# Attention's value projection as seven block products in a hand-written order

## The chip, the cores and the metric

One core of one Trainium2 chip runs the whole program. The metric is device time in microseconds (us) of one execution; lower is better. TensorE (PE) multiplies, VectorE (DVE), ScalarE (ACT) and GpSimd (POOL) do elementwise work, SyncE (SP) issues the transfers.

## The reference

Two pre-normalised residual layers on x of 512 frames by 1024 channels, each with a token mixer and a gated MLP. The first layer's mixer is a pooling mixer, the second's is attention of 16 heads of 64.

```python
for i in range(DEPTH):                      # DEPTH = 2
    h = rmsnorm(x, mix_norm[i])
    x = x + (pool_mixer if i == 0 else chunk_attention)(h, ...)
    h = rmsnorm(x, ffn_norm[i])
    x = x + (silu(causal_dwconv3(h @ w_gate)) * (h @ w_val)) @ w_out   # d_ff = 2816
...
qkv = h @ w_qkv                             # [512, 1024] x [1024, 3072]
q, k, v = jnp.split(qkv, 3, axis=-1)        # q and k are normalised by head
```

The change concerns v = h @ w_v, a product of 512 x 1024 by 1024 x 1024, and what stands just ahead of it and just behind it.

## The kernel before

Activations lie channel-major in `X[0..7]`, eight tiles of 128 channels by 512 frames in fp32. Every fp32 product is made from three products of rounded parts (`mm3`, lines 121 to 125): an operand is split into hi, a rounded copy made by ACT, and lo, the remainder made by DVE (`split`, lines 97 to 103; `split_scaled`, lines 105 to 108, the same with a scale), and hi x hi, hi x lo and lo x hi are added in PSUM. A matmul has a stationary operand of 128 x 128 and a moving one of 128 x 512.

**The end of the first layer.** `ffn` (line 382) makes the 2816 hidden channels in 22 tiles, most of them with seven block products in place of eight (`strassen`), and adds the output product in four groups of hidden tiles (`OUT`). The last group, `output(3)`, has five hidden tiles; for each of the eight output tiles d it makes 15 matmuls, for which a 128 x 640 weight is loaded, split (lines 409 and 410, one tile ahead) and consumed, and DVE adds the result onto `X[d]` (line 833). The hidden rows' two parts lie in slots `U`: four pairs in a pool and eight in `set1`. The groups take turns at two halves of `U`.

**The opening of attention.** `prepare` scales `X[k]` by the norm's gain and splits it into `XS` (which is `set2`, in the tiles `two`; lines 107 and 108), squares it on ACT (line 146) and lets POOL add the squares into `n_acc` (line 148). The factor of each frame is applied later, to the results. `project(0)` makes the first four heads' q and k in four PSUM banks with 96 matmuls, its weights loaded in four pieces of 512 KB (`load_split`). Then come the frames' factors (`frame_rstd`), the head norms, and four multiplications on POOL that apply them to `Z` (line 979). `values(0)` and `values(1)` make the halves of v, 96 matmuls each: for each of four pieces of 256 channels, eight groups of three matmuls, in which the lo part of the weights is used from the second matmul on. `evict` scales and splits the results out of PSUM into `set1`, 16 small steps on ACT and as many on DVE for each half (lines 107 and 108, tiles `one`). `channel_major(0, i)` transposes `Z` on PE, splits it and moves it by DMA. Then the heads begin, with the three other projections woven in; their lo parts are made by POOL (`project(1)`, line 103 on POOL).

**What sets the order.** Within `manual_schedule` an engine's instructions keep the order in which they are written. Before, that holds for PE in `ffn` and in the heads, and for DVE, ACT and SP in the middle of `ffn`; the opening of attention, and the output products of the last group on ACT and DVE, are ordered by a planner from priorities and estimated times. Weights' parts of all stages take turns in two buffers for hi and two for lo (`wh`, `wl`), loads in three (`wr`).

## Time and profile before

| what | value |
|---|---|
| median of 3 runs | 972.0 us (971.98 to 972.19) |
| the profiled execution's own time | 972.12 us |
| its span, from the first to the last instruction | 970.3 us |
| PE busy | 961.6 us, 99% of the span |
| PE's weight loads (PEld) | 815.0 us, 84% |
| DVE busy | 809.6 us, 83% |
| ACT busy | 576.6 us, 59% |
| POOL busy | 102.9 us, 11% |

Rows of the timeline give the start in us, the duration in us, the engine, the source line, the operation, output <- inputs, and the count; in brackets the idle time before it and what ended it. Rows that follow each other and are alike may be merged (x4), and a few matmuls are missing from a trace. A matmul's duration reaches over the start of the next one: the distance between starts is what one costs.

### The profile page before, as it was taken

What the parts mean: (1) busy time and instruction counts of PE and PEld (TensorE: products, weight loads), DVE (VectorE), ACT (ScalarE), POOL (GpSimd) and SP (SyncE); (2) the same over time, 40 slices, a digit from 0 to 9 for tenths busy, and PEclk for the clock granted to TensorE, in tenths of its full rate; (3) what the DMA queues carried; (4) which work ended last, traced back from release to release, by engine and by line L of the source; (5) the groups of instructions that cost most, each with busy time, mean ns of one, the idle gap of its engine ahead of it and who ended that gap; (6) DMA issues with size and microseconds to landing.
All of it is one profiled execution on the core that took longest, in us unless ns stands there. A gap on an engine that the chain in (4) does not pass through costs nothing.

```text
span 970.3 us, 13704 instructions
## 1 busy us (share of the span) xinstructions
PE 961.6 (99%) x4982; PEld 815.0 (84%) x4982; DVE 809.6 (83%) x1462; ACT 576.6 (59%) x990; POOL 102.9 (11%) x90
## 2 busy tenths in 40 slices
PE   8999999999999999999999999999999999999998
PEld 7788988888888888888888787888988888888886
DVE  8999999999899854442777888999999999989953
ACT  7665564655555544345898988646565565566531
POOL 2300000000000013204534532000000000000000
PEclk9999999999999999999999999999999999999999
DMA  9222332332323224232343341332233233332323
GB/s 342 77 93 71 114 113 75 120 120 92 105 76 120 78 84 147 94 121 91 111 115 107 97 118 55 101 108 80 94 114 104 87 120 108 104 103 77 116 79 109
DMA packets 37427, 102.82 MB, mean 106 GB/s; under 512 B 4432, under 2 KB 7904, under 8 KB 37360
## 3 DMA queue, kind: packets, MB, share of 16 engines
q1 hardware_dynamic: 37296, 101.90, 33.0%
q8 instruction: 39, 0.64, 0.3%
q14 instruction: 28, 0.23, 0.1%
q0 software_dynamic: 32, 0.04, 0.0%
q10 hardware_dynamic: 32, 0.00, 0.0%
HBM read 95.60 MB, written 2.14 MB: 101 GB/s over the span
## 4 chain that ended last, share of the span: by engine, by line
PE 94%; DVE 4%; ACT 2%; issue 0%; DMA 0%; DVEq 0%; ACTq 0%
PE st_m L610 11%; PE out L124 8%; PE out L123 8%; PE out L125 8%; PE st_m L612 6%; PE st_t L610 6%; PE gv L124 4%; PE gv L123 4%; PE gv L125 4%; PE qk L124 3%; PE qk L123 3%; PE qk L125 3%; PE st_t L612 3%; PE st_b L610 3%; PE tp L1078 2%; PE oo L1090 2%
## 5 line engine op out<-in xcount | busy, mean ns | idle before, releaser
L124 PE MATMUL out<-one,ow_h 128*128 128x512 f32 x224 | 87.9, 393 | 0.0
L123 PE MATMUL out<-one,ow_h 128*128 128x512 f32 x224 | 87.8, 392 | 0.0
L125 PE MATMUL out<-one,ow_l 128*128 128x512 f32 x224 | 87.8, 392 | 0.0
L833 DVE TENSOR_TENSOR X<-out,X 128x512 f32<-128x512 f32 (+1 forms) x65 | 44.1, 680 | 49.1 <-PE out L125 48.9
L409 ACT ACTIVATE ow_h<-wo_r 128x640 fp32r<-128x640 f32 (+1 forms) x64 | 50.4, 788 | 56.4 <-PE out L124 46.8
L610 PE MATMUL st_m<-two,g_h 128*128 128x512 f32 x240 | 75.1, 394 | 0.0
L610 PE MATMUL st_m<-h,g_h 128*128 128x512 f32 x240 | 74.0, 389 | 0.0
L410 DVE TENSOR_TENSOR ow_l<-wo_r,ow_h 128x640 fp32r<-128x640 f32 (+1 forms) x64 | 56.5, 883 | 2.5 <-ACT ow_h L409 2.5
L424 DVE SCALAR_TENSOR_TENSOR c<-a,col,c 128x511 f32<-128x511 f32 (+1 forms) x76 | 56.3, 743 | 0.0
L610 PEld LDWEIGHTS st_m<-h,g_h 128*128 128x128 f32 x240 | 45.1, 188 | 10.3
L612 PEld LDWEIGHTS st_m<-two,g_l 128*128 128x128 f32 x240 | 45.0, 188 | 9.5
L610 PEld LDWEIGHTS st_m<-two,g_h 128*128 128x128 f32 x240 | 44.0, 188 | 10.4 <-ACT w L619 0.8
L619 ACT ACTIVATE w<-st_m 128x512 f32<-128x512 f32 x30 | 17.9, 598 | 56.8 <-PE st_m L612 56.8
L125 PE MATMUL qk<-wqk_h,two 128*128 128x512 f32 x128 | 51.4, 402 | 0.0
L123 PE MATMUL qk<-wqk_h,two 128*128 128x512 f32 x128 | 50.8, 409 | 0.0
L124 PE MATMUL qk<-wqk_l,two 128*128 128x512 f32 x128 | 50.8, 397 | 0.0
L612 PE MATMUL st_m<-h,g_l 128*128 128x256 f32 x240 | 48.3, 283 | 0.0
L125 PEld LDWEIGHTS out<-one,ow_l 128*128 128x128 f32 x224 | 42.3, 189 | 6.3
L124 PEld LDWEIGHTS out<-one,ow_h 128*128 128x128 f32 x224 | 42.3, 189 | 6.3 <-DVE one L435 0.3
L612 PE MATMUL st_m<-two,g_l 128*128 128x256 f32 x240 | 47.6, 280 | 0.0
L123 PEld LDWEIGHTS out<-one,ow_h 128*128 128x128 f32 x224 | 42.3, 189 | 6.0
L1066 DVE CUSTOM_DVE_ANT_0 sb<-sc,B 128x128 f32<-128x128 f32 (+1 forms) x64 | 31.1, 486 | 18.9 <-PE sc L1063 18.1
(378 smaller groups left out, 2928.6 us busy)
## 6 DMA issues: line engine op xcount, KB each, us to landing
gv_r<-gv SPq DMA_DIRECT2D x86, 512.0 KB, 3.9
wo_r<-wout SPq DMA_DIRECT2D x32, 384.0 KB, 3.1
wo_r<-wout SPq DMA_DIRECT2D x32, 320.0 KB, 2.9
wqk_r<-wqk SPq DMA_DIRECT2D x16, 512.0 KB, 3.4
wv_r<-wv SPq DMA_DIRECT2D x8, 512.0 KB, 3.3
wo_r<-wo SPq DMA_DIRECT2D x8, 512.0 KB, 3.4
xt<-xt SPq DMA_DIRECT2D x4, 512.0 KB, 5.1
X<-xT SPq DMA_DIRECT2D x8, 256.0 KB, 7.4
```

Of the source, the lines that this page charges most:

```text
L123: yield nc.tensor.matmul(o, sh, mh, start=first, stop=False, **how)
L124: yield nc.tensor.matmul(o, sh, ml, start=False, stop=False, **how)
L125: yield nc.tensor.matmul(o, sl, mh, start=False, stop=last, **how)
L409: nc.scalar.activation(hi[:, :n], raw[:, :n], AF.Copy)
L410: return hi, lo, lambda: nc.vector.tensor_sub(lo[:, :n], raw[:, :n], hi[:, :n].bitcast(F32))
L424: nc.vector.scalar_tensor_tensor(c[:, j:], a[:, :S - j], cw[2 - j], c[:, j:], op0=OP.mult, op1=OP.add)
L610: nc.tensor.matmul(o, hi[:, c], B[i, name], start=first and i == 0, stop=False, **how)
L612: nc.tensor.matmul(o[:, 0], lo[:, c], B[i, name][:, 0], start=False, stop=i == 3, **how)
L833: nc.vector.tensor_add(X[d][:, fs], o[:, fs], X[d][:, fs])
L1066: nc.vector.tensor_tensor_reduce(out=s_[:, :n], in0=sc[:, :n], in1=BT[h % 2][:, :n][:, ::-1], scale=1.0, scalar=3e38, op0=OP.add, op1=OP.m ...
L1078: nc.tensor.transpose(tp[:, j * P:(j + 1) * P], s_[:, j * P:(j + 1) * P], ident)
L1090: nc.tensor.matmul(oo[:, j * P:], V[j, h // 4][:, h % 4].rearrange("p a d -> p (a d)"), PT[e][c][:, 4 * j:3 * j + TT].rearrange("p t q -> ...
```

## The change

The 1024 x 1024 product is cut into blocks of two by two: frames into halves (256 each), channels into even and odd tiles of 128, output columns into halves of 512. Seven block products take the place of eight (Winograd's form). Their left sides are a11, a12, a22 and four sums s1 to s4 of blocks of the scaled activations; their right sides are b11, b21 and b22, and four differences t1 to t4 of blocks of the weights, made by DVE in the loaded tiles. b22 is loaded a second time, since t2 is made in its place.

- The sums s1 to s4 (`frame_sums`, on DVE, 256 frames wide) and their parts (`forms_hi`, `forms_lo`) are made between the last output products of the first layer, through a hook in `output` (`after`, `amid`). `ffn` returns before the last group's products, and `opening` runs them. The parts go into `set1`, so the groups of the first layer's `ffn` take their slots the other way round, and the last one uses the pool's four pairs, which now lie in a pool of their own.
- The scaled activations get an fp32 copy (`Y`), from which hi is made. The squares are added by DVE and no longer by POOL.
- Each product is made in two halves of 12 matmuls (`half`): 8 with the hi part of the weights, then 4 with the lo part.
- Results are added up in SBUF (`x1`, `y6`, `y5`, `c12`) and from there scaled and split into `set1` (`store`).
- One order is written out for PE, DVE, ACT and SP, from the last output products to the last store.
- Pools: weight blocks and sums lie in a pool (`pre`) that closes ahead of the heads' tiles; three pools wait tile by tile.

The functions `frame_sums`, `forms_hi`, `half`, `after` and the order that is written out:

```diff
-    def prepare(XS, c, name):
-        acc = g_tile(f"{name}_acc")
-        for k in range(KD):
-            split_scaled(X[k], col[:, c + k:c + k + 1], XS[k], XS[KD + k])
-        for k in range(KD):
-            sumsq(k, acc, name)
...
+    def ffn(l, first, pool, acc, summed=None, upool=None, hook=None):
+        U = [tuple((upool or pool).tile([P, S], F32R, name=f"u{j}{c}") for c in "hl") for j in range(2 * GM - KD)]
         U += [(set1[j], set1[KD + j]) for j in range(KD)]
-        slot = {f: U[f - b + GM * (g % 2)] for g, (b, n) in enumerate(OUT) for f in range(b, b + n)}
+        slot = {f: U[f - b + GM * (g % 2 if hook is None else 1 - g % 2)] for g, (b, n) in enumerate(OUT) for f in range(b, b + n)}
...
+            last = hook is not None and g == len(OUT) - 1
             def halves(d):
-                w.append(parts(asked.pop((g, d)), m * P, f"ow{l}_{g}_{d}", True, True))
+                raw = asked.pop((g, d))
+                if last:
+                    hi, lo = (wp.tile([P, 1024], F32R, name=f"ow{l}_{g}_{d}_{c}", tag=f"w{c}", bufs=2) for c in "hl")
+                    nc.scalar.activation(hi[:, :m * P], raw[:, :m * P], AF.Copy)
+                    w.append((hi, lo, lambda: nc.vector.tensor_sub(lo[:, :m * P], raw[:, :m * P], hi[:, :m * P].bitcast(F32))))
+                else:
+                    w.append(parts(raw, m * P, f"ow{l}_{g}_{d}", True, True))
...
+                if last and d:
+                    hook["after"](d - 1)
                 o = psum("Q", f"out{l}_{g}_{d}")
                 for i in range(m):
+                    if last and i == 2:
+                        hook["amid"](d)
...
+            PAIRS, ONE, FOUR = ((4, 5), (10, 11), (14, 15), (0, 1)), (9, 12, 13, 8), (2, 3, 6, 7)
+            halves = slice(0, HALF), slice(HALF, S)
+            def scaled(k):
+                Y[k] = g_tile(f"y{k}")
+                nc.scalar.activation(Y[k], X[k], AF.Copy, scale=gain(k))
+                nc.scalar.activation(XS[k], Y[k], AF.Copy)
+                SQ[k] = g_tile(f"n1_sq{k}")
+                nc.scalar.activation(SQ[k], X[k], AF.Square)
+            def low(k):
+                nc.vector.scalar_tensor_tensor(XS[KD + k], X[k], gain(k), XS[k].bitcast(F32), op0=OP.mult, op1=OP.subtract)
+            def add_square(k):
+                nc.vector.tensor_add(SQ[0], SQ[0], SQ.pop(k))
+            def frame_sums(m):
+                ye, yo = Y.pop(2 * m), Y.pop(2 * m + 1)
+                (a11, a21), (a12, a22) = ([y[:, h] for h in halves] for y in (ye, yo))
+                sums[m] = vx(f"s23_{m}"), vx(f"s14_{m}")
+                (s2, s3), (s1, s4) = ([x[:, h] for h in halves] for x in sums[m])
+                nc.vector.tensor_add(s1, a21, a22)
+                nc.vector.tensor_sub(s3, a11, a21)
+                nc.vector.tensor_sub(s2, s1, a11)
+                nc.vector.tensor_sub(s4, a12, s2)
+            def forms_hi(m):
+                s23, s14 = sums[m]
+                h23, l23 = (set1[j] for j in PAIRS[m])
+                one, four = set1[ONE[m]], set1[FOUR[m]]
+                nc.scalar.activation(h23, s23, AF.Copy)
+                for x, h in zip((one, four), halves):
+                    nc.scalar.activation(x[:, :HALF], s14[:, h], AF.Copy)
+                form["s2", m], form["s3", m] = ((h23[:, h], l23[:, h]) for h in halves)
+                form["s1", m], form["s4", m] = ((x[:, :HALF], x[:, HALF:]) for x in (one, four))
+            def forms_lo(m):
+                s23, s14 = sums.pop(m)
+                h23, l23 = (set1[j] for j in PAIRS[m])
+                nc.vector.tensor_sub(l23, s23, h23.bitcast(F32))
+                for x, h in zip((set1[ONE[m]], set1[FOUR[m]]), halves):
+                    nc.vector.tensor_sub(x[:, HALF:], s14[:, h], x[:, :HALF].bitcast(F32))
...
+            def part_hi(key):
+                part[key] = [wp.tile([P, 1024], F32R, name=f"{key}_{c}", tag=f"w{c}", bufs=2) for c in "hl"]
+                nc.scalar.activation(part[key][0], raws[key], AF.Copy)
+            def part_lo(key):
+                nc.vector.tensor_sub(part[key][1], raws[key], part[key][0].bitcast(F32))
...
+            def t4(j):
+                nc.vector.tensor_sub(blocks["b21", j], blocks["b21", j], blocks["b22", j])
+            SEQ = ("b11", "b21", "b22", "b11", "b12", "b21", "b22")
...
+            def after(d):
+                if d in (3, 5):
+                    forms_hi((d - 3) // 2)
+                scaled(d)
+                if d == 6:
+                    part_hi("q0")
+                if d == 1:
+                    low(0)
+                if d == 2:
+                    low(1)
+                if d > 1:
+                    add_square(d - 1)
+                if d in (2, 4, 6):
+                    frame_sums(d // 2 - 1)
+                if d in (3, 5):
+                    forms_lo((d - 3) // 2)
+                if 3 < d < KD - 1:
+                    ask(d - 4)
+                if d > 3:
+                    for n in (("b11", "b12"), ("b22",), ())[d - 4]:
+                        for j in range(2):
+                            block(n, j)
+            def amid(d):
+                if d == KD - 1:
+                    part_lo("q0")
+            hook["after"], hook["amid"] = after, amid
+            run(rest)
...
+            def half(n, o, name, first):
+                z, j = divmod(n, 2)
+                h, l = part.pop(f"v{n}")
+                how = {"skip_group_check": not first}
+                for c in range(2):
+                    s = slice(c * S, (c + 1) * S)
+                    for i in range(2):
+                        sh, sl = stationary(name, 2 * j + c, i)
+                        nc.tensor.matmul(o[i], sh, h[:, s], start=first and n % 2 == 0 and c == 0, stop=False, **how)
+                        nc.tensor.matmul(o[i], sl, h[:, s], start=False, stop=False, **how)
+                for i in range(2):
+                    for c in range(2):
+                        sh, _ = stationary(name, 2 * j + c, i)
+                        nc.tensor.matmul(o[i], sh, l[:, c * S:(c + 1) * S], start=False, stop=j == 1 and c == 1, **how)
+            forms_hi(2)
+            ask(3)
+            for j in range(2):
+                block("b21", j)
+            part_hi("q1")
+            scaled(7)
+            low(2)
+            low(3)
+            part_lo("q1")
+            add_square(6)
+            forms_lo(2)
+            add_square(7)
+            frame_sums(3)
+            project(0)
+            part_hi("q2")
+            forms_hi(3)
+            low(4)
+            low(5)
+            part_lo("q2")
+            forms_lo(3)
+            t1(0)
+            project(1)
+            part_hi("q3")
+            low(6)
+            low(7)
+            part_lo("q3")
+            t1(1)
+            t2(0)
+            project(2)
+            st = psum("P", "n1_st")
+            for t in range(TT):
+                nc.tensor.matmul(st[:, t:t + 1], SQ[0][:, t * P:(t + 1) * P], ones, start=True, stop=True)
+            a, rcol, t_ = (small(f"n1_{c}", TT) for c in "ayt")
+            nc.vector.tensor_scalar(a, st[:, :TT], 1.0 / D, EPS, op0=OP.mult, op1=OP.add)
+            nc.scalar.activation(t_, a, AF.Ln)
+            nc.scalar.activation(rcol, t_, AF.Exp, scale=-0.5)
+            hi(0)
+            t2(1)
+            nc.vector.scalar_tensor_tensor(t_, rcol, -0.5, rcol, op0=OP.mult, op1=OP.mult)
+            nc.vector.tensor_mul(t_, t_, a)
+            nc.vector.scalar_tensor_tensor(rcol, t_, 1.5, rcol, op0=OP.add, op1=OP.mult)
+            nc.vector.scalar_tensor_tensor(r2, rcol, 1.0 / HD, rcol, op0=OP.mult, op1=OP.mult)
+            lo(0)
+            project(3)
...
+            def store(src, t, h):
+                for hh in range(2):
+                    V[t, 2 * h + hh] = vt = set1[(t * 2 + h) * 2 + hh].rearrange("p (h a d) -> p h a d", h=4, a=2)
+                    v4 = src[:, hh * 256:(hh + 1) * 256].rearrange("p (h d) -> p h d", d=HD)
+                    for e in range(2):
+                        split_scaled(v4[:, e::2, :], rcol[:, t:t + 1], vt[:, e::2, e, :], vt[:, e::2, 1 - e, :])
...
+            hi(1)
+            nc.vector.tensor_copy(flat[1], ov[1])
+            nc.scalar.activation(flat[0], ov[0], AF.Copy)
+            nc.scalar.activation(flat[2], ov[2], AF.Copy)
+            nc.vector.tensor_copy(flat[3], ov[3])
+            square(0)
+            lo(1)
+            half(0, A, "a11", True)
+            hi(2)
+            for t in range(1, TT):
+                square(t)
+            reduce(0)
+            lo(2)
+            reduce(1)
+            t3(0)
+            half(1, A, "a11", True)
+            x1 = pair_of("x1")
+            for i in range(2):
+                copy(x1, A, i)
+            hi(3)
+            reduce(2)
+            reduce(3)
+            lo(3)
+            nc.vector.tensor_mul(by_frame(a), by_frame(ss), r2[:, :, None].to_broadcast([P, TT, 8]))
+            nc.vector.tensor_scalar(a, a, EPS, None, op0=OP.add)
+            B = [psum("P", f"vb{i}") for i in range(2)]
+            half(2, B, "a12", True)
+            hi(4)
+            nc.scalar.activation(t_, a, AF.Ln)
+            nc.scalar.activation(y, t_, AF.Exp, scale=-0.5)
+            lo(4)
+            t3(1)
+            nc.vector.scalar_tensor_tensor(t_, y, -0.5, y, op0=OP.mult, op1=OP.mult)
+            nc.vector.tensor_mul(t_, t_, a)
+            nc.vector.scalar_tensor_tensor(y, t_, 1.5, y, op0=OP.add, op1=OP.mult)
+            nc.vector.tensor_mul(by_frame(y), by_frame(y), rcol[:, :, None].to_broadcast([P, TT, 8]))
+            for t in range(TT):
+                nc.gpsimd.tensor_mul(Z[0, t], Z[0, t], by_frame(y)[:, t, :, None].to_broadcast([P, 8, HD]))
+            half(3, B, "a12", True)
+            hi(5)
+            lo(5)
+            add(x1, B)
+            half(4, A, "s2", False)
+            hi(6)
+            lo(6)
+            t4(0)
+            half(5, A, "s2", False)
+            hi(7)
+            y6 = pair_of("y6")
+            for i in range(2):
+                copy(y6, A, i)
+            lo(7)
+            t4(1)
+            C = [psum("S", f"vc{i}", 4) for i in range(2)]
+            half(6, C, "s3", True)
+            hi(8)
+            lo(8)
+            for j in range(2):
+                blocks["b22", j] = load(source(1, 1, j), f"b22r_{j}")
+            channel_major(0, 0)
+            half(7, C, "s3", True)
+            hi(9)
+            lo(9)
+            channel_major(0, 1)
+            add(y6, C)
+            store(x1[0], 0, 0)
+            half(8, A, "s1", False)
+            hi(10)
+            lo(10)
+            store(x1[1], 1, 0)
+            half(9, A, "s1", False)
+            hi(11)
+            y5 = pair_of("y5")
+            for i in range(2):
+                copy(y5, A, i)
+            lo(11)
+            B = [psum("P", f"vd{i}") for i in range(2)]
+            half(10, B, "a22", True)
+            hi(12)
+            lo(12)
+            add(y5, C)
+            store(y5[0], 2, 1)
+            half(11, B, "a22", True)
+            hi(13)
+            lo(13)
+            add(y6, B)
+            store(y5[1], 3, 1)
+            half(12, A, "s4", False)
+            store(y6[0], 2, 0)
+            half(13, A, "s4", False)
+            c = pair_of("c12")
+            nc.scalar.activation(c[0], A[0], AF.Copy)
+            nc.vector.tensor_copy(c[1], A[1])
+            store(y6[1], 3, 0)
+            for i in range(2):
+                store(c[i], i, 1)
+            return rcol
...
-            yield from products(ov, wqk[c], f"wqk{c}", nc.gpsimd if c else None, evict)
-            if c == 0:
-                rcol = frame_rstd(acc, "n1")[0]
-                nc.vector.scalar_tensor_tensor(r2, rcol, 1.0 / HD, rcol, op0=OP.mult, op1=OP.mult)
+            yield from products(ov, wqk[c], f"wqk{c}", nc.gpsimd, evict)
...
-        def values(half, banks):
...
-        run(project(0, "SS"))
-        while late:
-            late.pop(0)()
-        run(values(0, "PQ"))
-        for i in range(2):
-            channel_major(0, i)
-        run(values(1, "SS"))
+        r2, late = small("r2", TT), []
+        closing = ExitStack()
+        with tc.tile_pool(name="pre", bufs=1, reuse_waits="tile") as pre:
+            with tc.manual_schedule(engines={ET.PE, ET.DVE, ET.Activation, ET.SP}):
+                rcol = opening(pre)
...
+    hidden_slots, hook = ExitStack(), {}
+    upool = hidden_slots.enter_context(tc.tile_pool(name="bu", bufs=1, side="right"))
     with tc.tile_pool(name="b0", bufs=1) as big:
-        ffn(0, first, big, acc0)
-    with tc.tile_pool(name="ba", bufs=1) as big:
-        rest = attention()
+        rest = ffn(0, first, big, acc0, None, upool, hook)
+    with tc.tile_pool(name="ba", bufs=1, reuse_waits="tile") as big:
+        rest = attention(rest, hook, hidden_slots)
...
```

122 lines of the change are left out of this document (87 added, 35 removed).

## Prediction

> **What bounds the kernel now.** First the page: the shares, the slices and the chain that ended last.
>
> ```profile
> span 970.3 us, 13704 instructions
> PE 961.6 (99%) x4982; PEld 815.0 (84%) x4982; DVE 809.6 (83%) x1462; ACT 576.6 (59%) x990; POOL 102.9 (11%) x90
> PEclk9999999999999999999999999999999999999999
> PE 94%; DVE 4%; ACT 2%; issue 0%; DMA 0%; DVEq 0%; ACTq 0%
> ```
>
> TensorE is the bound from end to end, at full granted clock, so a matmul taken away counts unless something else comes late in its place. Second, the timeline of PE and DVE where the change lies: product 3 of the first layer's last output group, a stretch of the value products (two rows, ten matmuls apart inclusive), the one wait among them, and the first matmul of the next projection.
>
> ```profile
> 357.57 0.39 PE L123 MATMUL out<-one,ow_h 128*128 128x512 f32 x1
> 440.01 0.39 PE L124 MATMUL v<-wv_l,two 128*128 128x512 f32 x1
> 442.05 0.39 PE L125 MATMUL v<-wv_h,two 128*128 128x512 f32 x1
> 430.91 1.20 PE L123 MATMUL v<-wv_h,two 128*128 128x512 f32 x4
> 432.50 0.40 PE L125 MATMUL v<-wv_h,two 128*128 128x512 f32 x1
> 430.89 2.58 DVE L103 TENSOR_TENSOR wv_l<-wv_r,wv_h 128x1024 fp32r<-128x1024 f32 x2 [4.38 <-ACT wv_h L102]
> 442.27 0.39 PE L123 MATMUL qk<-wqk_h,two 128*128 128x512 f32 x1
> ```
>
> Ten matmuls begin within 442.05 - 440.01 = 2.04 us, nine steps: one costs 0.227 us, not the 0.39 of its own duration, since they overlap. From 357.57 to 442.27 are 84.7 us; they hold 75 output matmuls, 96 of the first projection and 192 for the values, 363 x 0.227 = 82.3. At 430.91 four matmuls and one that the merged rows leave out should have led to the sixth at 432.05; it begins at 432.50, so a wait of 0.45 us for a lo part lies here. The rest is transposes and the frame sums of squares.
>
> **The matmuls taken away.** Seven block products have 2 frame tiles x 4 channel tiles x 3 = 24 matmuls each: 168 in place of 192, each 128x512 as before. That is 24 x 0.227 = 5.44 us less on the bound engine. The old wait goes too, if lo parts used last are in time: 0.45. The Trainium skill, "TensorE: Matmul & The Clock Gate", section "Back-to-back issue gap", gives about 131 ns for a sustained matmul of 512 columns; by it the 24 would be worth an estimated 3.1 us and the whole sum below would come out 2.3 us weaker, but the rows show 227 ns, and I go by them.
>
> **What the change puts in front of PE: the last output products.** From here DVE and ScalarE follow one written order. Five rows that follow each other on DVE give the step from one operation to the next; the rows behind them ScalarE's steps, a pair of 256-wide DVE operations, and a pair that depend on each other.
>
> ```profile
> 368.99 0.68 DVE L833 TENSOR_TENSOR X<-out,X 128x512 f32<-128x512 f32 x1
> 369.59 0.81 DVE L410 TENSOR_TENSOR ow_l<-wo_r,ow_h 128x640 fp32r<-128x640 f32 x1
> 370.32 1.21 DVE L103 TENSOR_TENSOR wqk_l<-wqk_r,wqk_h 128x1024 fp32r<-128x1024 f32 x1
> 371.46 0.74 DVE L108 SCALAR_TENSOR_TENSOR two<-X,col,two 128x512 fp32r<-128x512 f32 x1
> 372.12 0.68 DVE L833 TENSOR_TENSOR X<-out,X 128x512 f32<-128x512 f32 x1
> 357.77 0.69 DVE L833 TENSOR_TENSOR X<-out,X 128x512 f32<-128x512 f32 x1 [1.16 <-PE out L125]
> 365.29 0.72 ACT L107 ACTIVATE two<-X,col 128x512 fp32r<-128x512 f32 x1 [0.17 <-DVE X L833]
> 365.92 0.62 ACT L146 ACTIVATE n_sq<-X 128x512 f32<-128x512 f32 x1
> 366.44 1.04 ACT L102 ACTIVATE wqk_h<-wqk_r 128x1024 fp32r<-128x1024 f32 x1
> 60.30 0.42 DVE L508 TENSOR_TENSOR t<-ha 128x256 f32<-128x256 f32 x1
> 60.63 0.41 DVE L510 TENSOR_TENSOR t<-hh,ha 128x256 f32<-128x256 f32 x1
> 400.27 0.17 DVE L137 SCALAR_TENSOR_TENSOR n_t<-n_y 128x4 f32<-128x4 f32 x1 [0.51 <-ACT n_y L136]
> 400.47 0.16 DVE L138 TENSOR_TENSOR n_t<-n_t,n_a 128x4 f32<-128x4 f32 x1
> ```
>
> So X's add steps 0.60, a 640-wide lo 0.73, a 1024-wide one 1.14, a scaled lo 0.66, a 256-wide sum 0.33, or 0.46 where the next needs its result (0.42 and the 0.03 that the last two rows leave between them). A product is 15 x 0.227 = 3.40 us. Before, DVE had 0.60 + 0.73 + 0.66 = 1.99 us in each and sat idle for 1.16 of it. Now the adds of squares come from GpSimd to DVE, and the frame sums come in. During product 3 DVE has X's add, a scaled lo, an add of squares (0.60, as X's add), four sums (0.33 + 0.33 + 0.46 + 0.33 = 1.45), and only then the lo of product 4. X's add begins 0.20 after the product before it has ended (357.57 and 357.77), so that lo is ready 0.20 + 0.60 + 0.66 + 0.60 + 1.45 + 0.81 = 4.32 us after product 3 began. PE loads it with the third matmul of product 4, at 3.40 + 0.23 = 3.63: **a wait of 0.7 us**. Products 4, 5 and 6 give DVE 0.60 + 0.60 + 1.26 + 0.73 = 3.19 (forms' lo parts 0.60 + 2 x 0.33), 3.38 and 3.19, within 3.40: no more there.
>
> The first projection's weights were split early before (366.44). Now the hi part of the first waits on ScalarE behind X[6]'s three passes: X[6] is added 0.9 us into product 7, the scaled copy steps 0.63, the copy and the square 0.52 each, then hi 1.04, at 3.6; the lo behind it 1.21, at 4.9 with the gaps. PE's second matmul of the projection wants it at 3.63: **1.3 us**. Behind this wait stand all matmuls, since PE's order is written out. From there to the values DVE is 1 us or more ahead of each use, by the same steps.
>
> **During the seven products.** A half is 12 x 0.227 = 2.72 us. DVE has for the fourteen: 14 lo parts x 1.14, 4 block differences x 1.14, 8 adds from PSUM x 0.60, 7 copies and reductions x 0.60, 3 scaled lo parts x 0.66, and 20 store operations x 0.33 that come before the last half's end: 38.1 us, some 40 with the small ones, beside 14 x 2.72 = 38.1. It keeps up because it starts ahead and because lo parts are used last: eight matmuls, 1.8 us, into a half. The tightest are the lo parts of halves 10 and 11, behind the adds and stores, about 1 us early; I take 0, bounds 0 and 1. ScalarE has 1.04 + 1.3 per half at most: no wait.
>
> Q's normalised rows are the next thing. GpSimd's four multiplications must be done before the transposes behind half 6.
>
> ```profile
> L979 POOL TENSOR_TENSOR z<-z,qk_y x16: 1037/1045/2087, 403.0 to 556.1; 128x512 f32<-128x512 f32 x16
> 404.00 1.23 DVE L103 TENSOR_TENSOR wv_l<-wv_r,wv_h 128x1024 fp32r<-128x1024 f32 x1 [1.10 <-ACT wv_h L102]
> 403.05 5.09 POOL L979 TENSOR_TENSOR z<-z,qk_y 128x512 f32<-128x512 f32 x4 [21.61 <-DVE qk_y L977]
> 513.89 1.55 DVE L103 TENSOR_TENSOR two<-o,two 128x512 fp32r<-128x512 f32 x1
> 513.85 4.50 POOL L979 TENSOR_TENSOR z<-z,qk_y 128x512 f32<-128x512 f32 x4 [5.56 <-DVE qk_y L977]
> ```
>
> One takes 1.04 us, but 2.09 where a two-input DVE operation lay across it; and at 513.89 a DVE operation that takes 0.68 took 1.55. They shut each other out, whole operations at a time. The Trainium skill, "GPSIMD Engine Reference", section "1. Specifications", says the same of DVE instructions with two SBUF inputs; it speaks against this change, which crowds DVE where before one such operation ran. The factors come 1.8 us after half 3 ends (behind a lo and a block difference, 2.28, and four small operations); half 6 ends 8.2 after it, the fourth transpose 0.35 later. So 6.7 us are there for 4.2. With two lo parts and a difference let in between, 4.2 + 3 x 1.14 = 7.6: **0.8 us late**. Bounds: 0 if nothing is shut out; 4.3 if DVE's row of lo(6), t4, lo(7), t4, lo(8) all goes first.
>
> **The next projection's first weights.**
>
> ```profile
> 437.03 1.06 ACT L102 ACTIVATE wqk_h<-wqk_r 128x1024 fp32r<-128x1024 f32 x1 [4.82 <-PE v L125]
> 438.59 2.39 POOL L103 TENSOR_TENSOR wqk_l<-wqk_r,wqk_h 128x1024 fp32r<-128x1024 f32 x1 [15.01 <-ACT wqk_h L102]
> 439.86 2.98 ACT L107 ACTIVATE one<-v,n_y 128x128 fp32r<-128x128 f32 x9 [0.42 <-DVE one L108]
> 373.66 0.39 PE L125 MATMUL qk<-wqk_h,two 128*128 128x512 f32 x1
> 373.89 0.39 PE L123 MATMUL out<-one,ow_h 128*128 128x512 f32 x1
> ```
>
> Before, the buffers came free a 24-matmul step ahead, and the lo was ready 1.5 us before its use (442.50). A half is only 12 matmuls: GpSimd can begin 0.2 us into the last half and ends 2.39 later, in time by a hair. But it now meets DVE's stores, which read SBUF and no longer PSUM, and a last copy out of PSUM queued behind four of them. Bounds 0 and 2 (a store queue held for 2.39); I take 0.2.
>
> Other moves: 12 loads of 512 KB go on SP within some 20 us; the page's first slice moved 342 GB/s, by which 6.3 MB take 18, each some 2 us ahead of its split; the two loads repeated have 30 us of cover. GpSimd loses the adds of squares, off PE's path. The first tiles of the layer's hidden rows now go into set1, which its opening products read: these last begin at 53.35, the first such row comes at 74.1. The heads after the values have the same work.
>
> ```profile
> 53.35 0.39 PE L125 MATMUL gv<-one,two 128*128 128x512 f32 x1
> L433 ACT ACTIVATE u0h<-c x4: 632/634/635, 74.1 to 787.4; 128x512 fp32r<-128x512 f32 x4
> GB/s 342 77 93 71 114 113 75 120 120 92 105 76 120 78 84 147 94 121 91 111 115 107 97 118 55 101 108 80 94 114 104 87 120 108 104 103 77 116 79 109
> ```
>
> **Sum.** -5.44 - 0.45 + 0.7 + 1.3 + 0.8 + 0.2 = -2.9 us on the profiled execution's 972.1 (span 970.3 and 1.8 around it), 969.2; it lies 0.1 above the median of 972.0, so I forecast 969.1.
>
> **Rivals.** *The covers hold*: ScalarE or DVE reach q0's split and the sums sooner, and GpSimd slips between. For it: DVE's idle 1.16 per product before. Against it: the sums of steps. Then all 5.9 count: 966.1. Chance 0.17.
>
> *GpSimd is shut out*: DVE's row goes first as a block, 4.3 in place of 0.8, and PE stands at the transposes behind half 6: 972.6; half of that, or a late copy at the end, gives 970.1 to 971.5. For it, the 2.09; against it, the 1.55, where GpSimd went first. Chance 0.18, all of it no change.
>
> *ScalarE's written order ends last* (slower): the hi part of the next projection's first weights stands behind the last stores. After the last half come a copy (0.6), twelve stores' hi (2.98 / 9 = 0.33 each, 4.0), hi 1.06, GpSimd 2.39: 8.3 us after the last product, and PE has nothing else: 969.1 + 8.1 = 977.2. It decides slower from 4.9 us on. For it: ScalarE's order is one block now. Against it: at 373.66 and 373.89 a matmul of free order stands between ones of written order, so an instruction from outside can be put into such a block. Chance 0.10.
>
> *The change does not do what it says* (still 192 matmuls): the code has fourteen halves of 12; 0.01, no change.
>
> **How the numbers follow.** Forecast 0.54, with a range of its own of 967.8 to 970.0. About 0.2% (1.9 us, from 970.1 to 973.9) is what a measurement here can tell from no change. Faster is 0.54 + 0.17 = 0.71; the same 0.18 + 0.01 = 0.19; slower 0.10. The range goes from the covers' 966.1 to 971.5, into the second rival; left out are the slower case and its upper part.
>
> **What would show it.** In the profile after: 168 matmuls into va, vb, vc and vd; PE waiting for ow_l about 0.7 at the fifth output product, for q0's lo about 1.3 at the projection's start, for z at the transposes about 0.8; no wait for lo parts within the halves. Wrong it would be if PE waits within the halves, or at the next projection for ScalarE, or if the span falls by over 5 us.

## The result, and the profile after

The changed kernel takes 975.0 us (973.62 to 976.16, 7 runs) where the kernel before takes 972.06 (971.96 to 972.55): a ratio of 1.0028, 95% interval 1.0017 to 1.0040. It is slower, by 2.9 us; the forecast was 969.1 with a range that ended at 971.5. The page of the profiled execution (974.83 us), its shares, clock slices and chain:

```profile
span 973.0 us, 13739 instructions
PE 959.5 (99%) x4958; PEld 811.5 (83%) x4958; DVE 849.5 (87%) x1520; ACT 593.5 (61%) x1023; POOL 96.5 (10%) x83
PEclk9999999999999999999999999999999999999999
PE 92%; DVE 5%; ACT 2%; issue 1%; DMA 0%; DVEq 0%
```

TensorE has 24 matmuls fewer (4958 for 4982) and 2.1 us less busy time, yet the span is 2.7 longer; DVE, with 40 us more work, now has 5% of the chain for 4%. Nothing more can be seen at this scale: a slice of 24 us hides what follows. So next the timeline, first of the part that the prediction worked out in detail (start, duration, engine, line, then what it waited for):

```profile
354.71 0.69 DVE L828 TENSOR_TENSOR X<-out,X 128x512 f32<-128x512 f32 x1 [2.07 <-PE out L125]
358.20 0.69 DVE L828 TENSOR_TENSOR X<-out,X 128x512 f32<-128x512 f32 x1 [1.41 <-PE out L125]
361.73 0.40 PE L124 MATMUL out<-u0l,ow_h 128*128 128x512 f32 x1
362.41 0.50 PE L125 MATMUL out<-u0h,ow_l 128*128 128x512 f32 x1 [0.28 <-DVE ow_l L798]
375.78 0.39 PE L125 MATMUL out<-one,ow_l 128*128 128x512 f32 x1
376.35 0.51 PE L123 MATMUL qk<-q_h,two 128*128 128x512 f32 x1 [0.18 <-ACT q_h L989]
377.61 0.50 PE L124 MATMUL qk<-q_l,two 128*128 128x512 f32 x1 [0.75 <-DVE q_l L992]
412.76 6.84 POOL L1209 TENSOR_TENSOR z<-z,qk_y 128x512 f32<-128x512 f32 x4 [79.31 <-DVE qk_y L1207]
419.26 0.72 PE L1352 MATMUL zt<-ident,z 128*128 128x128 f32 x4
428.88 1.22 DVE L992 TENSOR_TENSOR v_l<-b,v_h 128x1024 fp32r<-128x1024 f32 x1
430.29 1.09 PE L1094 MATMUL vd<-v_l,two 128*128 128x512 f32 x4
439.39 0.39 PE L123 MATMUL qk<-wqk_h,two 128*128 128x512 f32 x1
```

The next projection begins at 439.39, where it began at 442.27 before. Up to here the change gives 2.88 us, where the forecast's terms without the entry come to 3.1. What follows is the timeline of all engines around that point, and then one row of windows from each kernel (length, busy time of PE, PEld, DVE, ACT and POOL, then the granted clock, the share of its full speed that TensorE was given, the DMA share and GB/s), the first of before, the second of after.

```profile
434.05 1.28 ACT L107 ACTIVATE one<-y,n_y 128x128 fp32r<-128x128 f32 x4 [2.50 <-DVE y L1160]
435.24 1.05 ACT L989 ACTIVATE v_h<-b22r 128x1024 fp32r<-128x1024 f32 x1
437.36 1.05 ACT L102 ACTIVATE wqk_h<-wqk_r 128x1024 fp32r<-128x1024 f32 x1
438.54 4.78 POOL L103 TENSOR_TENSOR wqk_l<-wqk_r,wqk_h 128x1024 fp32r<-128x1024 f32 x2 [12.89 <-ACT wqk_h L102]
438.65 6.38 DVE L108 SCALAR_TENSOR_TENSOR one<-y,n_y,one 128x128 fp32r<-128x128 f32 x8
439.48 1.04 ACT L102 ACTIVATE wqk_h<-wqk_r 128x1024 fp32r<-128x1024 f32 x1
440.96 0.50 PE L124 MATMUL qk<-wqk_l,two 128*128 128x512 f32 x1 [1.18 <-POOL wqk_l L103]
442.68 0.39 PE L125 MATMUL qk<-wqk_h,two 128*128 128x512 f32 x1
444.96 0.68 DVE L1264 COPY c<-va 128x512 f32<-128x512 f32 x1
445.69 0.80 PE L123 MATMUL qk<-wqk_h,two 128*128 128x512 f32 x1 [2.62 <-DVE c L1264]
446.29 0.63 PE L124 MATMUL qk<-wqk_l,two 128*128 128x512 f32 x1
448.84 0.40 PE L124 MATMUL qk<-wqk_l,two 128*128 128x512 f32 x1
```

```profile
440.00:450.00 10.00, 10.00 (x46) 8.28 (x45) 4.71 (x15) 6.55 (x17) 4.28 (x3) 1.00 0.35 107
```

```profile
440.00:450.00 10.00, 6.41 (x21) 4.85 (x22) 8.78 (x21) 4.62 (x14) 3.47 (x4) 0.83 0.50 166
```

Within ten microseconds TensorE stands still twice and then runs slow. Against its step of 0.227 the matmul at 440.96 is 1.34 us late, and the step behind it 0.11 too long: 1.45. The one at 445.69 is 2.78 late (445.69 - 442.68 - 0.23). From there to 448.84 eight matmuls come in 3.15 us, where 7 steps take 1.59: 1.56 more, at steps of 0.43 and a granted clock of 0.83 over the window. In sum 5.79 us; the first matmul of the first head's mix comes 32.60 us behind the start of this projection before (442.27 to 474.87), and 38.39 after (439.39 to 477.78): the same 5.79 more. All of the loss lies here.

Why the copy at 444.96 is so late can be read on three engines. GpSimd does the lo parts of the first two weight pieces back to back, 4.78 us, at its usual 2.39 each. During them DVE is at the eight stores in front of the copy: 6.38 us. The merged row hides how they are spread; two of the eight stand out:

```profile
438.65 2.40 DVE L108 SCALAR_TENSOR_TENSOR one<-y,n_y,one 128x128 fp32r<-128x128 f32 x1
440.98 2.48 DVE L108 SCALAR_TENSOR_TENSOR one<-y,n_y,one 128x128 fp32r<-128x128 f32 x1
```

The other six take 0.34 each, about the 0.35 that such a store had in the kernel before. So DVE isn't idle in the profile: it is "busy" for 2.4 us with one small store beside the first GpSimd operation, and again with one beside the second.

### The profile page after: what moved, and what is told of

Same layout as the page of the kernel before. It is cut to its first block, busy times and chain, and to the rows that moved or that the text cites. A ratio compares the mean times of both kernels' runs of the same rounds, so it can differ in the third digit from the quotient of the medians.

```text
span 973.0 us, 13739 instructions
## 1 busy us (share of the span) xinstructions
PE 959.5 (99%) x4958; PEld 811.5 (83%) x4958; DVE 849.5 (87%) x1520; ACT 593.5 (61%) x1023; POOL 96.5 (10%) x83
## 4 chain that ended last, share of the span: by engine, by line
PE 92%; DVE 5%; ACT 2%; issue 1%; DMA 0%; DVEq 0%
PE st_m L593 11%; PE out L125 8%; PE out L124 8%; PE out L123 8%; PE st_m L595 6%; PE st_t L593 6%; PE gv L124 4%; PE gv L123 4%; PE gv L125 4%; PE qk L123 3%; PE qk L124 3%; PE qk L125 3%; PE st_t L595 3%; PE st_b L593 3%; DVE one L108 2%; PE tp L1398 2%
## 5 line engine op out<-in xcount | busy, mean ns | idle before, releaser
L392 ACT ACTIVATE ow_h<-wo_r 128x768 fp32r<-128x768 f32 (+1 forms) x56 | 44.5, 794 | 43.4 <-PE out L124 40.9
L393 DVE TENSOR_TENSOR ow_l<-wo_r,ow_h 128x768 fp32r<-128x768 f32 (+1 forms) x56 | 49.9, 891 | 2.1 <-ACT ow_h L392 2.1
L404 ACT ACTIVATE c<-a,col 128x512 f32<-128x512 f32 x38 | 30.7, 812 | 23.2 <-DVE a L751 21.6
L123 PE MATMUL qk<-wqk_h,two 128*128 128x512 f32 x96 | 40.7, 424 | 2.6 <-DVE c L1264 2.6
L1388 ACT ACTIVATE sb<-sb,mx 128x128 f32<-128x128 f32 (+1 forms) x64 | 35.7, 557 | 10.4 <-DVE mx L1386 9.9
```

The source lines that it names most:

```text
L123: yield nc.tensor.matmul(o, sh, mh, start=first, stop=False, **how)
L392: nc.scalar.activation(hi[:, :n], raw[:, :n], AF.Copy)
L393: return hi, lo, lambda: nc.vector.tensor_sub(lo[:, :n], raw[:, :n], hi[:, :n].bitcast(F32))
L404: nc.scalar.activation(c, a, AF.Identity, scale=cw[2], bias=cw[3])
L1388: nc.scalar.activation(s_[:, :n], s_[:, :n], AF.Exp, scale=-1.0, bias=mx[:, 0:1], accum_out=mx[:, 1:2])
```

## The experiments

Theory A: GpSimd's lo operations and DVE's stores, which read both operands from SBUF since the change, shut each other out; the copy out of PSUM stands behind the stores in DVE's written order, TensorE behind the copy, and the standstill brings the clock down. Rival B: DVE and ScalarE are simply behind with the stores. Times of the kernel before beside these runs are 972.0 to 972.3.

**The copy on ScalarE.**

```diff
-            nc.vector.tensor_copy(c[1], A[1])
+            nc.scalar.activation(c[1], A[1], AF.Copy)
```

> In the changed kernel the copy of the second half of the last value product out of PSUM (c[1], DVE, line 1264) ended at about 444.9 us, behind eight store operations that took 6.38 us on DVE, and TensorE waited 2.62 us for it; just after, 9 matmuls ran at half the granted clock (0.43 us a step). Here this one copy is an ACTIVATE on ScalarE at the same place of the written order; nothing else changes. Theory A (GpSimd's two 1024-wide lo operations and DVE's stores from SBUF shut each other out, and the copy merely stands behind those stores): the 2.6 us wait and the slow matmuls behind it go, DVE's eight stores still take about 6 us, the 1.2 us wait for GpSimd's lo stays; 975.0 - 2.6 - 1.5 = about 971 us. Rival B (DVE and ScalarE are simply behind with the stores, with no shutting out): ScalarE's copy comes late as well, since it stands behind the same ping-pong; half of the wait or more is left, 973 to 975 us.

Measured: 970.79 us (11 runs), ratio to before 0.9987 (0.9978 to 0.9995). Twelve stores, the copy and the wait that is left, in the timeline of the profiled execution (972.5, the slowest of the eleven):

```profile
440.62 7.46 DVE L108 SCALAR_TENSOR_TENSOR one<-y,n_y,one 128x128 fp32r<-128x128 f32 x12
442.87 0.57 ACT L1264 ACTIVATE c<-va 128x512 f32<-128x512 f32 x1
442.95 0.50 PE L124 MATMUL qk<-wqk_l,two 128*128 128x512 f32 x1 [1.14 <-POOL wqk_l L103]
```

As theory A has it: the stores are as slow as before (four more in 1.08 us), nobody waits for them, no matmul runs at half clock. Rival B is wrong about ScalarE.

**GpSimd out of the entry.** The lo parts of the first two pieces are ScalarE copies of the raw weights; their subtraction is left out.

```diff
-                hi, lo = load_split(w[kk], 1024, f"{name}_{kk}", eng=eng)
+                if name == "wqk1" and kk < 2:
+                    ...
+                    nc.scalar.activation(hi, raw, AF.Copy)
+                    nc.scalar.activation(lo, raw, AF.Copy)
+                ...
```

> The lo parts of the first two weight pieces of the next projection are here plain ScalarE copies of the raw weights: the subtraction of hi is left out for these two (a part of the computation is changed), so GpSimd does nothing at the entry into the next projection and ScalarE does two more 1024-wide copies. Theory A (shutting out): DVE's eight stores go back from 6.38 us to about 8 x 0.28 = 2.2 us, the copy of c[1] is through by about 441.5, TensorE's wait for it goes from 2.6 to under 0.5, the wait for a lo part becomes at most 1 us of ScalarE; no half clock; 969 to 970.5 us. Rival B (DVE's backlog alone): the eight stores still end at about 445, the wait for c[1] stays near 2.6; 973.5 to 975 us.

Measured: 970.39 us, 0.9980 (0.9970 to 0.9989).

```profile
439.18 2.25 DVE L108 SCALAR_TENSOR_TENSOR one<-y,n_y,one 128x128 fp32r<-128x128 f32 x8
441.35 0.68 DVE L1264 COPY c<-va 128x512 f32<-128x512 f32 x1
442.08 0.50 PE L123 MATMUL qk<-wqk_h,two 128*128 128x512 f32 x1 [0.59 <-DVE c L1264]
```

The same eight stores take 2.25 us without GpSimd and 6.38 with it. So 4.13 us of them were standing still while GpSimd worked for 4.78, and no single store takes over 0.35 here. The copy is still 0.85 us late (0.75, and 0.11 on the step behind it). The Trainium skill, "SBUF — State Buffer", section "SBUF: two separate sides", calls the port pair that the two share an exclusive lock, held for a whole instruction; this pair of rows agrees, and so does the slowness of GpSimd's four multiplications above, 6.84 us where four alone take 4.2. Rival B falls: the backlog is GpSimd's doing.

**GpSimd with copies.** In place of each of the two subtractions, which are left out, GpSimd makes a copy, with one input from SBUF.

```diff
+            ...
+            nc.scalar.activation(hi, raw, AF.Copy)
+            nc.gpsimd.tensor_copy(lo, raw)
+            ...
```

> The changed kernel with the copy on DVE as it is, but GpSimd's two lo operations at the entry are copies of the raw weights (one input from SBUF in place of two; the subtraction is left out for these two pieces, so a part of the computation is changed). Theory A1 (only operations with two inputs from SBUF on both sides shut each other out): DVE's eight stores go from 6.38 to about 2.3 us, the wait for the copy from 2.6 to about 0.6, 970.5 to 971.5 us. Theory A2 (any GpSimd operation on SBUF holds such a DVE operation): the stores stay at 5 to 6.4 us, the wait at 2 or more, 973.5 to 975 us.

Measured: 970.31 us, 0.9982 (0.9973 to 0.9992).

```profile
438.15 1.49 POOL L117 CAST wqk_l<-wqk_r 128x1024 fp32r<-128x1024 f32 x1 [11.32 <-PE va L1102]
439.85 2.97 DVE L108 SCALAR_TENSOR_TENSOR one<-y,n_y,one 128x128 fp32r<-128x128 f32 x8
440.81 1.07 POOL L117 CAST wqk_l<-wqk_r 128x1024 fp32r<-128x1024 f32 x1 [1.18 <-PE va L1102]
440.90 1.13 DVE L108 SCALAR_TENSOR_TENSOR one<-y,n_y,one 128x128 fp32r<-128x128 f32 x1
```

The time is A1's, and still the rows speak for A2. The first GpSimd copy ended at 439.64, before the first store, and met none. Beside the second, one store takes 1.13 us, as long as that copy, and the other seven 0.35 at most. So a copy holds a store too; it costs little here because it is short (1.07 for 2.39) and only one of the two met the stores.

**The copies first.** Both copies keep their engines and are written before the last twelve stores.

```diff
             add(y6, B)
-            store(y5[1], 3, 1)
             half(12, A, "s4", False)
-            store(y6[0], 2, 0)
             half(13, A, "s4", False)
             c = pair_of("c12")
             nc.scalar.activation(c[0], A[0], AF.Copy)
             nc.vector.tensor_copy(c[1], A[1])
+            store(y5[1], 3, 1)
+            store(y6[0], 2, 0)
             store(y6[1], 3, 0)
```

> The copies of the last value product stay on the engines that the change gave them (ScalarE and DVE), but both are written ahead of the last twelve stores, not behind eight of them. If the copy's place behind stores that GpSimd holds up is what made TensorE wait 2.6 us, moving it on DVE alone is as good as moving it to ScalarE: the copy ends by about 440.2 us, TensorE wants it at about 440.8, no half clock, 970.0 to 971.0 us, with 0.5 to 1.2 us of wait left for GpSimd's lo. Rival (DVE is too full there in any order; ScalarE's help was needed): 973 us or more.

Measured: 969.69 us (10 runs), 0.9975 (0.9966 to 0.9985).

```profile
437.58 4.86 POOL L103 TENSOR_TENSOR wqk_l<-wqk_r,wqk_h 128x1024 fp32r<-128x1024 f32 x2 [11.72 <-ACT wqk_h L102]
439.80 0.69 DVE L1262 COPY c<-va 128x512 f32<-128x512 f32 x1 [0.86 <-PE va L1094]
440.76 4.71 DVE L108 SCALAR_TENSOR_TENSOR one<-y,n_y,one 128x128 fp32r<-128x128 f32 x12 [0.27 <-ACT one L107]
```

The order alone does it, and a little more: DVE's copy, which reads PSUM, takes its usual 0.69 in the middle of GpSimd's subtractions; ScalarE, with no stores ahead, reaches the hi part earlier, so the wait for GpSimd's lo shrinks from 1.45 to 0.34 (the matmul at 440.07 is 0.24 late, the next 0.10). For that reason the time is 0.3 under the range expected.

**The price of a standstill.** In the kernel before, the lo subtraction of three value pieces is repeated.

```diff
+        for _ in range(again):
+            nc.vector.tensor_sub(lo[:, :n], raw[:, :n], hi[:, :n].bitcast(F32))
...
+                again = {"wv0_2": 3, "wv1_0": 4, "wv1_2": 6}.get(f"{name}_{kk}", 0)
```

> The kernel before, with the lo subtraction of three of its value weight pieces repeated 3, 4 and 6 times on DVE, so that TensorE, which waits for these lo parts, stands still for about 1, 2.4 and 4 us at three places some 10 us apart (the result is unchanged). It asks for the price of a standstill by itself. If the half clock after the entry was caused by the standstill (1.2 + 2.6 us within 6 us), matmuls at 0.43 us steps follow the longest gap here for about 2 to 4 us, and none or fewer the 1 us gap: the time grows by the gaps (about 7 us) and 1.5 to 3 more. If the half clock has another cause (the load of DMA or of the other engines there), the granted clock stays at 1.00 behind all three, and the time grows by the gaps alone.

Measured: 987.72 us, one run. Standstills of 0.7, 4.65 and 5.37 us; windows of five microseconds around the first, the second and the third:

```profile
410.00:415.00 5.00, 4.08 (x21) 3.03 (x20) 4.99 (x5) 1.30 (x3) 2.74 (x3) 1.00 0.37 129
425.00:430.00 5.00, 2.43 (x6) 1.95 (x7) 4.17 (x11) 1.62 (x5) 0.00 (x0) 0.57 0.58 186
430.00:435.00 5.00, 5.00 (x18) 3.98 (x17) 0.00 (x0) 0.17 (x1) 0.00 (x0) 0.74 0.06 25
445.00:450.00 5.00, 3.71 (x10) 2.95 (x11) 1.22 (x1) 0.00 (x0) 0.00 (x0) 0.66 0.39 125
```

Half clock follows the two long ones, also with DMA at 0.06 and the other engines idle (430 to 435), and not the short one. It costs 2.4 and 1.6 us beyond the standstill.

A second run of this kind was to try about 2.4 and 3.1 us:

> As the run with three standstills (0.6, 4.65 and 5.4 us: the two long ones were followed by 2.4 and 1.6 us lost at half clock), now with two shorter ones, by 2 and 4 repeats of a 1.14 us lo subtraction less: about 2.4 us and about 3.1 us alone, some 18 us apart; the result is unchanged. In the changed kernel 2.78 us, 3 us behind one of 1.45, was followed by 1.5 us lost. If one standstill of that size is enough, half clock follows both here (or the longer one); if it took the two together, the granted clock stays at 1.00.

Measured: 980.75 us, one run, and a miss: the first pair of repeats was hidden, and the second made one standstill of 6.50 us, followed by 2.7 us lost at half clock. It says nothing on the shorter ones.

**The standstill by itself, at its place.** In the kernel with the copies first, DVE's copy eight times over.

```diff
+            for _ in range(8):
-            nc.vector.tensor_copy(c[1], A[1])
+                nc.vector.tensor_copy(c[1], A[1])
```

> The kernel with both copies ahead of the stores (969.7 us, a wait of only 0.34 us there), with the DVE copy of the second tile written eight times over (the result is unchanged): seven more, 0.6 us each, so that TensorE waits for it about 2.7 us, as in the changed kernel, but without the 1.45 us standstill 3 us ahead of it. If one standstill of 2.7 us is enough for half clock, matmuls at 0.43 us steps follow it, some 1.5 us lost: 969.7 + 2.7 + 1.5 = about 974 us. If it took the two together, the clock stays at 1.00: about 972.4 us. If the standstill is given back by more slack behind it, under 971.

Measured: 974.91 us (973.03 to 976.00, 10 runs), 5.2 more than with one copy.

```profile
441.47 0.39 PE L125 MATMUL qk<-wqk_h,two 128*128 128x512 f32 x1
445.26 0.80 PE L123 MATMUL qk<-wqk_h,two 128*128 128x512 f32 x1 [3.41 <-DVE c L1263]
445.86 0.63 PE L124 MATMUL qk<-wqk_l,two 128*128 128x512 f32 x1
448.30 0.40 PE L124 MATMUL qk<-wqk_l,two 128*128 128x512 f32 x1
```

The copies step 0.72, not 0.60, so the standstill is 3.56 us and not 2.7. Half clock follows it without a shorter one in front: 445.26 to 448.30 holds 1.4 us more than 7 steps. Eight of the ten executions took 974.3 to 976.0 at a mean clock of 0.996 to 0.998; the other two took 973.0 and 973.2 at 1.000, which is 969.7 and the standstill alone. So the clock's part in those eight is about 2.0 us (1.2 to 2.9). Whether 2.78 alone is enough stays open; the changed kernel had 1.45 in front of it. The Trainium skill, "TensorE: Matmul & The Clock Gate", section "What's actually happening", gives about 3.4 us of idleness for the drop to half clock, and as much of activity for the return. The 3.56 fits; 2.78 and 1.45 within six microseconds are under that figure and had the drop too, and no wait of up to 1.8 us in any run was followed by it. The return took 3.0 (here) to 5.7 us.

**The first part alone: q0 early.** The order of work is kept but for three places: the first projection piece is split before X[6]'s passes, its lo comes before the frame sums, and the first two scaled lo parts come one product earlier.

```diff
-                scaled(d)
                 if d == 6:
                     part_hi("q0")
-                if d == 1:
-                    low(0)
-                if d == 2:
-                    low(1)
+                scaled(d)
+                if d < 2:
+                    low(d)
                 if d > 1:
                     add_square(d - 1)
+                if d == 6:
+                    part_lo("q0")
...
```

> Only the order in the last output products is changed: the first projection piece is split before X[6]'s three ScalarE passes, its lo comes before the frame sums, and the first two scaled lo parts come one product earlier. Both theories put the slowness at the entry into the next projection and not here: the waits of 1.48 us for q0 and 0.56 us for the output weights' lo go, all else stays; 975.0 - 1.5 to 2.0 = 973.0 to 973.5 us, with the waits of 1.2 and 2.6 us at the entry and the half clock behind them unchanged. If the early waits were not on the path (given back later), the time stays at 975.

Measured: 973.39 us (971.48 to 974.45, 11 runs), 1.0008 (0.9999 to 1.0017): 1.6 less than the change. Of TensorE's waits between 340 and 460 us two are left, 2.6 us for DVE's copy and 1.2 for GpSimd's lo. What is won early isn't given back. Together with the copy on ScalarE:

> The copy on ScalarE and the earlier q0 together. The changed kernel's 975.0 went to 970.8 with the first alone and to 973.4 with the second alone. If the two waits are separate, the gains add: 975.0 - 4.2 - 1.6 = 969.2 us, with only the wait of about 1.1 us for GpSimd's lo left. If the earlier values only run into the entry sooner (given back), 970.5 or more.

Measured: 968.59 us (5 runs), 0.9964 (0.9952 to 0.9977); of TensorE's waits between 340 and 460 us only the 1.2 us for GpSimd's lo are left.

**Lo parts in turn.** The other half of the change undone, on top of the copy on ScalarE.

```diff
                         nc.tensor.matmul(o[i], sh, h[:, s], start=first and n % 2 == 0 and c == 0, stop=False, **how)
-                        nc.tensor.matmul(o[i], sl, h[:, s], start=False, stop=False, **how)
-                for i in range(2):
-                    for c in range(2):
-                        sh, _ = stationary(name, 2 * j + c, i)
-                        nc.tensor.matmul(o[i], sh, l[:, c * S:(c + 1) * S], start=False, stop=j == 1 and c == 1, **how)
+                        nc.tensor.matmul(o[i], sh, l[:, s], start=False, stop=False, **how)
+                        nc.tensor.matmul(o[i], sl, h[:, s], start=False, stop=j == 1 and c == 1, **how)
```

> The other half of the change undone: in each product half the weights' lo part is used in turn (hi, lo, hi for each channel tile, as in the other products) and not in the last four matmuls; with the copy on ScalarE, against whose 970.8 us it stands. By the changed kernel's trace the lo part of halves 3, 7, 10, 11 and 13 ends 0.6 to 1.4 us after the second matmul of its half would want it (half 10: ready at 430.10 us, wanted at 428.71). Theory (lo used last is what covers DVE): TensorE waits within halves, 1.5 to 3 us in sum, since a wait once taken also lets DVE catch up; 972.3 to 973.8 us. Rival (DVE is ahead enough, the order within a half is worth nothing): 970.8 us, no wait over 0.2 us in a half.

Measured: 975.86 us, 1.0038 (1.0026 to 1.0051), 5.1 over the 970.8 of the kernel it stands against. Its waits between 340 and 460 us that the copy on ScalarE alone doesn't have, and that for GpSimd (line waited for: total, times, longest):

```profile
PE qk L124 <- POOL wqk_l L103: 2.0, 2, 1.6
PE vd L1090 <- DVE v_l L992: 1.2, 1, 1.2
PE vb L1090 <- DVE v_l L992: 0.8, 1, 0.8
PE va L1090 <- DVE v_l L992: 0.8, 1, 0.8
```

Lo last is worth 5.1 us here, nearly the 5.44 of the matmuls taken away: 4.0 within the halves (the late starts and the steps behind them, which come to more than the waits that the view gives), where up to 3 were expected, and 1.1 by a second wait for GpSimd at the entry.

**All three.** Both copies on ScalarE ahead of the stores, q0 early, and the next projection's first piece split in the written order, its lo on DVE, so that GpSimd has one operation there and not two. The lo stores of `y5[0]` go behind the copies as well.

```diff
...
+            raws["w0"] = load(wqk[1, 0], "wqk1_0")
+            late5 = store(y5[0], 2, 1, True)
             half(12, A, "s4", False)
+            part_hi("w0")
+            part_lo("w0")
+            ready["wqk1_0"] = part["w0"]
             half(13, A, "s4", False)
             c = pair_of("c12")
+            for i in range(2):
+                nc.scalar.activation(c[i], A[i], AF.Copy)
...
+            store(y5[1], 3, 1)
...
```

> The changed kernel with three things at once: both copies of the last value product on ScalarE, written before the stores; the first projection's pieces split earlier as in the run with the earlier q0; and the first weight piece of the next projection split inside the written order, its lo by DVE before the last stores, so that GpSimd does only the second piece's lo at the entry. Computation unchanged. Theory A (the loss is three waits, each with its own cause): 975.0 less 2.6 (the copy), 1.5 (the half clock), 1.2 (GpSimd's lo) and 1.6 to 2.0 (q0 and the output weights' lo) = 967.5 to 968.5 us, no wait of TensorE over 0.3 us between 360 and 450 us. Rival (the waits cover one another, or DVE's stores, now 24 of them behind the entry, make a wait of their own for the second piece's lo or for the heads): 969 to 971 us, no better than the copy on ScalarE with the earlier q0 alone.

Measured: 967.15 us (966.89 to 967.53, 5 runs), 0.9948 (0.9935 to 0.9960): 4.9 us faster than the kernel before and 7.8 than the change.

```profile
435.19 1.23 DVE L992 TENSOR_TENSOR w_l<-wqk,w_h 128x1024 fp32r<-128x1024 f32 x1
437.96 2.40 POOL L103 TENSOR_TENSOR wqk_l<-wqk_r,wqk_h 128x1024 fp32r<-128x1024 f32 x1 [14.20 <-ACT wqk_h L102]
439.12 4.28 DVE L108 SCALAR_TENSOR_TENSOR one<-y,n_y,one 128x128 fp32r<-128x128 f32 x12 [1.65 <-ACT one L107]
```

DVE's stores still stand still beside GpSimd's one lo (4.28 us for some 3.4; the one at 439.12 takes 1.39), and nothing waits for them; no matmul between 355 and 450 us is more than 0.1 us late.

The losses read from the changed kernel's trace account for the runs within 0.4 us. They are 0.56 (ow's lo), 1.48 (q0), 1.45 (GpSimd's lo), 2.78 (the copy) and 1.56 (half clock):

| kernel | 975.0 less or plus | gives | measured |
|---|---|---|---|
| copy on ScalarE | -2.78 - 1.56 | 970.7 | 970.8 |
| copies first | -2.78 - 1.56 - 1.45 + 0.34 | 969.6 | 969.7 |
| GpSimd out | all three at the entry, + 0.85 for the copy that is left | 970.1 | 970.4 |
| q0 early | -0.56 - 1.48 | 973.0 | 973.4 |
| copy and q0 | -2.78 - 1.56 - 0.56 - 1.48 | 968.6 | 968.6 |
| all three | all five | 967.2 | 967.2 |

## Why the prediction was wrong

It failed in one term, "**The next projection's first weights**": "Bounds 0 and 2 (a store queue held for 2.39); I take 0.2". It measured 5.8, and with 0.2 in its place the kernel would have come out at 969.4, inside the range. Point by point:

- *The matmuls taken away*: right. The groups by tile have 96 matmuls into va and 24 each into vb, vc and vd, 168 in all. The 0.45 of the old wait went too.
- *The wait for ow's lo in product 4*, forecast 0.7: 0.56 (362.41 - 361.73 less a step, and 0.11 on the next).
- *q0's split*, forecast 1.3: 1.48, of which 1.14 is for the lo part; the other 0.34 is for its hi part, on which the first matmul already waited.
- *GpSimd's multiplications*, forecast 0.8 late: under 0.1. They took 6.84 us where I had 7.6, and ended at 419.60. The four transposes begin at 419.26, 419.37, 419.48 and 419.66, so only the fourth was held, by some 0.07. The mechanism was right: three DVE operations were let in between, as forecast, for 2.64 us in place of 3.4.
- *During the seven products*, forecast 0 (bounds 0 and 1): 0, but thinner than I had it. The lo of half 10 ended at 430.10, 0.19 us before its first use, not "about 1 us early". The run with lo parts in turn shows what that order covers.
- A term that wasn't there: the last output group's products took 3.49 us each (354.71 to 358.20) and not 3.40: eight of them, 0.7 us. With the 0.15 us by which this execution was already late at the group's start, the sum to the entry is -5.44 - 0.45 + 0.56 + 1.48 + 0.07 + 0.7 + 0.15 = -2.9; measured -2.88. That this lies so near the forecast's 3.1 is in part luck: the 0.7 that GpSimd's multiplications cost less is made up by the 0.7 of a term that the sum didn't have.
- *The entry*. I had seen that GpSimd's lo "meets DVE's stores" and that "a last copy out of PSUM" is "queued behind four of them", and still bounded it by one operation of 2.39 us. Three things were missed. First, ScalarE puts the second piece's hi between its stores (the row at 439.48), as I had argued against the third rival, and so GpSimd has two operations in a row, not one; each held one store for its whole length (2.40 and 2.48 us), where the bound has one of 2.39. Second, the copy stands behind eight stores: the hi of half 13 came only at 435.24, since ScalarE's order has four stores ahead of it that waited 2.50 us for DVE (the row at 434.05), and with it DVE's lo, its adds and the four stores of y5 slipped; for the same reason the first hi came at 437.36 and GpSimd's lo 1.45 us too late, where I had it "in time by a hair". Third, a bound on a wait isn't a bound on its cost: the standstill brought the clock down.

Of the rivals, the one that gave GpSimd's shutting out 0.18 had the right mechanism at the wrong place and from the wrong side: it had GpSimd kept waiting by DVE. It also named "a late copy at the end", but at no more than 971.5. Its 4.3 doesn't follow from the five operations it lists: at 1.14 each they give 3.2 (971.5 us). The slower one, by ScalarE's written order, didn't come: the hi parts were put between the stores, as the argument against it said. (Its terms come to 8.05 us, not 8.3.) The sign of being wrong that the prediction named for this place was a wait for ScalarE; the waits were for GpSimd's lo and DVE's copy.

## What to carry to other kernels

A copy out of PSUM that frees a bank for the next stage belongs ahead of all stores in the written order; here that move is worth 5.3 us. Where an order is written out on some engines, look for what engines outside it will do at its end, in pairs and with one more operation than was there before, and price a queue by all that stands in front of the one operation that somebody waits for. When the bound engine has never stood still in the kernel before, add the clock to the price of any standstill of about three microseconds.

## What the runs showed of the hardware

- At the entry GpSimd's subtraction of 128x1024 keeps its 2.4 us beside DVE's stores. Each GpSimd operation that meets the stores holds one of them, which has two SBUF inputs, for as long as it lasts itself, and the store is shown as busy meanwhile: 2.40 and 2.48 us in the changed kernel, 1.13 beside a GpSimd copy, where the others take 0.34. Where DVE's operations are wide, the two take turns, and GpSimd waits as well (its four multiplications, 4.2 us to 6.84). DVE's copy out of PSUM beside GpSimd's subtraction takes its usual 0.69, and the stores of the kernel before, with one input from PSUM, take 0.35 beside GpSimd as elsewhere (those at 439.47, 440.26 and 440.61).
- Behind a standstill of 3.56 us the granted clock was halved in 8 of 10 executions, by their mean clock; behind 4.65, 5.37 and 6.50 us in the one execution each that was profiled. It cost 1.4 to 2.7 us more in those profiled. Behind the changed kernel's 1.45 and 2.78 it isn't certain either: five of its seven executions have a mean clock of 0.998, and the two at 973.6 and 973.8 have 0.999; with q0 early nine of eleven have 0.996 to 0.998, and the fastest, 971.5 at 0.999, is what the sum gives without half clock. That fits the spread of these two kernels' times over 2.5 and 3 us. The half clock needn't begin with the first matmul behind the wait either: in the profiled execution with q0 early TensorE starts again at 445.07, and the steps of 0.43 begin at 446.21.
- The output products' matmuls step 0.233 us in the changed kernel's last group where they stepped 0.227 before. The 0.233 isn't new: the first layer's first two output groups (90 to 268 us) step 0.233 in the kernel before as well. The cause wasn't tried and stays open.
